# A weight stream woven through seven-product pairs: its steps placed over 28 pair steps instead of 17

## Chip, cores and metric

The kernel runs on one core of a Trainium2 chip. The metric is the device time of one execution in microseconds (us). Three runs of the kernel before gave 883.15, 884.38 and 886.47 us; the median is 884.38 us.

## What is computed

Two layers of a trunk over 256 tokens of width 2048: first a gated linear recurrence with dilated attention, then gated linear attention with a spatial gating unit, and a last norm. The change lies in the second layer. Its input projection is one product with a wide weight matrix, whose columns are then split:

```python
h = rms_norm(x, norm)
z = h @ w_in
q, k, v, a_lr, gc, u, vd, gd = jnp.split(z, split_points(ODD_SIZES), axis=-1)
...
yc = rms_norm(o, head_norm).reshape(bsz, seq, GLA_VW).astype(x.dtype) * jax.nn.silu(gc)
yd = spatial_gating(jax.nn.gelu(u), jax.nn.gelu(vd), w_s, b_s, v_norm) * jax.nn.silu(gd)
return jnp.concatenate([yc.astype(x.dtype), yd.astype(x.dtype)], axis=-1) @ w_out
```

## The kernel before

Every weight passes the same road. SP issues a load of 512 KB (128 partitions by 1024 numbers of 4 bytes) into a raw tile. ACT casts it into a high part (line 138, `whi`), DVE subtracts that from the raw tile into a low part (line 73 by way of line 139, `wlo`), and PE makes three products per operand: high by high, high by low, low by high. The rings of the high and low parts (`hip`, `lop`) have four buffers each, so ACT and DVE can be up to four pieces ahead of PE. One such piece is called a step here.

Three times (for q and k, for vd, for u) two blocks of 512 columns are made by `pair`: seven block products instead of eight, with sums of blocks as operands. A pair has 28 steps, each a cast, a subtraction and 6 matmuls of 512 columns. I number them 1 to 28:

- Steps 1 to 4 use the pieces `x0`, steps 5 to 8 the pieces `y0`, 9 to 12 `x0` again, 13 to 16 `y0`, 17 to 20 `x0`. In steps 1 to 12, as soon as a piece has been cast and subtracted, an accumulating DMA on the POOL queue (line 245) adds another block's piece to it in place; the sum is used eight steps later. So there are twelve accumulating DMAs in a pair, in three groups of four.
- Steps 21, 22, 23 and 25 use four fresh pieces `z0`, loaded into the ring called raw; steps 24, 26, 27 and 28 use `x0[0]` to `x0[3]` after DVE has added `z0[i]` to each (line 299, "the additions"). An addition is pinned by `keep_in_program_order` behind the DVE instruction that stands before it in the program: the first addition stands after step 22, then after 24, 26 and 27. Each addition ends the use of a raw buffer.
- After step 20 DVE makes four small combinations from PSUM (lines 279 to 283), and at the end a fifth (line 301). The next pair's first pieces are fetched between steps 21 and 26 (`onward`).

Beside a pair runs `Stream`: four other column blocks (the gates gc and gd) at eight steps each. A step of the stream is one piece from the raw ring, which has three buffers in all for the stream and for `z0`, and 12 matmuls of 512 columns. `weave` runs a pair and, after each of its steps, as many steps of the stream as its rule says: 10 for the first pair, 8 for the second, 10 for the third; `stream.finish` (line 982) makes the last four. When eight steps are done, ACT reads the finished block with a Silu (lines 791 and 798).

The program's order gives priorities. The framework lays out each engine's queue from them and from what it takes to be ready, except where an order is pinned. Small tasks (`spawn`, `tick`) for attention and gating are laid between the steps, by counts of products.

Of the kernel before, what the change touches and what calls it, by code (L numbers as in the profile page):

```python
# [51 lines left out]
def trunk(ctx, tc, x, xt, lead, w_in0, w_out0, w_va, w_in1, w_out1, w_gate, small, dist, cst, w_alpha, w_s,  # L52
# [164 lines left out]
    def weave(steps, stream, count):  # L217

        done = taken = 0
        while True:  # L220
            try:
                next(steps)
            except StopIteration as end:
                return end.value
            taken += 1
            while done < count and done * 17 < taken * count:
                stream.step()
                done += 1

# [573 lines left out]
    paired[0] = True  # L803
    x0 = [fetch(w_in1, 6, i, "rx") for i in range(4)]
    ps, ps_k, x0 = weave(pair(w_in1, 6, 10, act2, forms2, x0, "ry", 14), stream, 10)
    drain()
    eb, enb, ebl = decays
# [81 lines left out]
    vf = []  # L889
    mv = tiny.tile([P, 8, 2], F32, name="mv", tag="mv", bufs=1)  # L890
    *vd, x0 = weave(pair(w_in1, 14, 18, act2, forms2, x0, "rx", 30), stream, 8)
    for c, ps in enumerate(vd):
        t = big_tile([P, 2, 512], f"vf{c}")
# [53 lines left out]
    def mix(c, t):  # L947
        yield 2
        for b in range(2):
# [7 lines left out]
            yield 2  # L957

    *ud, _ = weave(pair(w_in1, 30, 34, act2, forms2, x0, "ry"), stream, 10)
    paired[0] = False  # L960
    for c, ps in enumerate(ud):
# [172 lines left out]
```

## Time and profile before

| | |
|---|---|
| median of three runs | 884.38 us |
| the profiled execution | 882.66 us |
| its span in the trace | 881.0 us |
| PE busy | 857.9 us, 97% |
| DVE busy | 610.0 us, 69% |
| ACT busy | 526.3 us, 60% |
| first pair, first matmul | 537.4 us |
| last third-pair matmuls | about 770 us |

A busy PE is not a PE at its peak, since a matmul's duration overlaps the next one's. Within the pairs it is better read by the number of matmuls in a stretch.

### The profile page before, as it was taken

To read this page: it belongs to the slowest core of one execution; us is meant where nothing else is said; L and a number is where in the kernel's file an instruction comes from. 1 tells how busy PE (TensorE), PEld (TensorE's weight loads), DVE (VectorE), ACT (ScalarE), POOL (GpSimd) and SP (SyncE) were. 2 spreads that over 40 slices of the span, in tenths; PEclk is the share of its full clock that TensorE was granted. 3 is DMA by queue.
4 is the path that set the end of the run, shared out by engine and by line. 5 is a ranking of instruction groups with operands and counts; after the bars stand their busy time and mean duration, and the time that the engine had idled before them with its cause. 6 is when DMAs were issued, how large, how long until landed. Compare 5 with 4: busy or idle time off the path is not lost.

```text
span 881.0 us, 11887 instructions
## 1 busy us (share of the span) xinstructions
PE 857.9 (97%) x4408; PEld 718.6 (82%) x4408; DVE 610.0 (69%) x867; ACT 526.3 (60%) x764; POOL 42.9 (5%) x60
## 2 busy tenths in 40 slices
PE   8999999999999999999999999998999899899996
PEld 7888888888888888888888988885768578688886
DVE  7676557677576586666555996679748976995652
ACT  7755556666766766554444776565476766654532
POOL 1100000000000000010000002201210121000000
PEclk9999999999999999999999999999999999999999
DMA  9896555555455455565544658967965899665502
GB/s 342 335 366 213 185 194 164 170 169 177 160 177 170 144 172 178 190 208 194 184 135 154 219 184 209 252 225 211 250 144 176 245 254 322 202 220 189 190 2 96
DMA packets 50266, 175.53 MB, mean 199 GB/s; under 512 B 5648, under 2 KB 6160, under 8 KB 49952
## 3 DMA queue, kind: packets, MB, share of 16 engines
q1 hardware_dynamic: 43920, 152.65, 50.8%
q0 software_dynamic: 6144, 22.06, 12.6%
q8 instruction: 34, 0.56, 0.2%
q14 instruction: 24, 0.20, 0.1%
q10 hardware_dynamic: 144, 0.07, 0.0%
HBM read 172.66 MB, written 2.10 MB: 198 GB/s over the span
## 4 chain that ended last, share of the span: by engine, by line
PE 91%; DVE 6%; ACT 1%; issue 1%; DMA 0%; ACTq 0%
PE pc L315 20%; PE ps L147 15%; PE ps L148 15%; PE ps L146 15%; PE pc L314 10%; PE ps L251 3%; PE ps L252 3%; PE ps L253 3%; DVE wlo L73 3%; ACT whi L138 1%; DVE rx L299 1%; PE pc L317 1%; PE sc L500 1%; PE gp L584 1%; PE gp L583 1%
## 5 line engine op out<-in xcount | busy, mean ns | idle before, releaser
L315 PE MATMUL pc<-act,whi 128*128 128x512 f32 x768 | 269.8, 395 | 0.0
L314 PE MATMUL pc<-act,wlo 128*128 128x256 f32 x720 | 208.5, 290 | 0.0
L73 DVE TENSOR_TENSOR wlo<-rx,whi 128x1024 fp32r<-128x1024 f32 (+2 forms) x118 | 141.4, 1199 | 74.9 <-ACT whi L138 73.3
L138 ACT CAST whi<-rx 128x1024 fp32r<-128x1024 f32 (+1 forms) x115 | 119.9, 1044 | 100.3 <-PE ps L148 59.1
L73 DVE TENSOR_TENSOR wlo<-ry,whi 128x1024 fp32r<-128x1024 f32 (+2 forms) x110 | 131.6, 1198 | 67.9 <-ACT whi L138 66.7
L315 PEld LDWEIGHTS pc<-act,whi 128*128 128x128 f32 x768 | 142.6, 188 | 29.4
L138 ACT CAST whi<-ry 128x1024 fp32r<-128x1024 f32 (+1 forms) x108 | 112.2, 1041 | 90.4 <-PE ps L148 53.2
L73 DVE TENSOR_TENSOR wlo<-raw,whi 128x1024 fp32r<-128x1024 f32 (+2 forms) x100 | 119.0, 1190 | 47.7 <-ACT whi L138 45.7
L138 ACT CAST whi<-raw 128x1024 fp32r<-128x1024 f32 (+1 forms) x97 | 100.9, 1040 | 68.0 <-PE ps L148 25.6
L314 PEld LDWEIGHTS pc<-act,wlo 128*128 128x128 f32 x720 | 135.9, 189 | 2.4 <-DVE wlo L73 0.8
L146 PE MATMUL ps<-whi,act 128*128 128x512 f32 (+2 forms) x352 | 131.8, 377 | 1.4 <-DVE la_s L473 1.1
L147 PE MATMUL ps<-wlo,act 128*128 128x512 f32 (+2 forms) x352 | 131.0, 372 | 1.3 <-DVE wlo L73 1.2
L148 PE MATMUL ps<-whi,act 128*128 128x512 f32 (+2 forms) x352 | 130.7, 371 | 0.0
L146 PE MATMUL ps<-whi,yt 128*128 128x512 f32 (+1 forms) x256 | 97.3, 380 | 0.0
L148 PE MATMUL ps<-whi,yt 128*128 128x512 f32 (+1 forms) x256 | 96.4, 376 | 0.0
L147 PE MATMUL ps<-wlo,yt 128*128 128x512 f32 (+1 forms) x256 | 96.2, 376 | 0.0
L146 PEld LDWEIGHTS ps<-whi,act 128*128 128x128 f32 x352 | 66.1, 188 | 15.0 <-issue 2.2
L147 PEld LDWEIGHTS ps<-wlo,act 128*128 128x128 f32 x352 | 66.3, 188 | 13.5 <-DVE wlo L73 2.6
L148 PEld LDWEIGHTS ps<-whi,act 128*128 128x128 f32 x352 | 66.2, 188 | 11.4
L148 PEld LDWEIGHTS ps<-whi,yt 128*128 128x128 f32 x256 | 48.2, 188 | 8.9
L147 PEld LDWEIGHTS ps<-wlo,yt 128*128 128x128 f32 x256 | 48.2, 188 | 8.5
L146 PEld LDWEIGHTS ps<-whi,yt 128*128 128x128 f32 x256 | 48.2, 188 | 8.3
(289 smaller groups left out, 1040.1 us busy)
## 6 DMA issues: line engine op xcount, KB each, us to landing
raw<-in_w_in SPq DMA_DIRECT2D x77, 512.0 KB, 5.2
ry<-in_w_in SPq DMA_DIRECT2D x64, 512.0 KB, 4.7
rx<-in_w_in SPq DMA_DIRECT2D x63, 512.0 KB, 4.6
rx<-in_w_out SPq DMA_DIRECT2D x24, 512.0 KB, 4.3
ry<-in_w_out SPq DMA_DIRECT2D x23, 512.0 KB, 4.0
rx<-in_w_in POOLq DMA_DIRECT2D x20, 512.0 KB, 9.9
raw<-in_w_out SPq DMA_DIRECT2D x17, 512.0 KB, 4.5
ry<-in_w_in POOLq DMA_DIRECT2D x16, 512.0 KB, 8.6
```

What stands on the lines that cost most here:

```text
L73: nc.vector.tensor_tensor(out=o, in0=a, in1=hi.bitcast(F32), op=ALU.subtract)
L138: nc.scalar.copy(hi, raw)
L146: nc.tensor.matmul(ps[b], xh, wh, start=first, stop=False)
L147: nc.tensor.matmul(ps[b], xh, wl, start=False, stop=False)
L148: nc.tensor.matmul(ps[b], xl, wh, start=False, stop=last)
L251: nc.tensor.matmul(ps, xh, wh, start=(first and j == 0), stop=False, skip_group_check=not first)
L252: nc.tensor.matmul(ps, xh, wl, start=False, stop=False, skip_group_check=not first)
L253: nc.tensor.matmul(ps, xl, wh, start=False, stop=(j == 7), skip_group_check=not first)
L299: tc.keep_in_program_order(nc.vector.tensor_tensor(out=x0[i - 1], in0=z0[i - 1], in1=x0[i - 1], op=ALU.add))
L314: nc.tensor.matmul(ps[c][:, 1, :], wl, act[:, k, 0:T], start=False, stop=False)
L315: nc.tensor.matmul(ps[c], wh, act[:, k, :], start=(k == 0), stop=(k == KT - 1))
L317: nc.tensor.matmul(ps[c][:, 1, :], wl, act[:, k, 0:T], start=False, stop=False)
```

## The change

Only the rule of `weave` changes:

```diff
@@ -223,7 +223,7 @@
             except StopIteration as end:
                 return end.value
             taken += 1
-            while done < count and done * 17 < taken * count:
+            while done * 28 < taken * count:
                 stream.step()
                 done += 1
```

Worked out, steps of the stream stand after these steps of a pair:

| steps of the stream | before | after the change |
|---|---|---|
| 10 (first and third pair) | 1, 2, 4, 6, 7, 9, 11, 12, 14, 16 | 1, 3, 6, 9, 12, 15, 17, 20, 23, 26 |
| 8 (second pair) | 1, 3, 5, 7, 9, 11, 13, 15 | 1, 4, 8, 11, 15, 18, 22, 25 |

The numbers of steps stay, since at step 28 the new rule has run exactly `count` of them. The pinning of the additions stands in both kernels.

## Rows read from the trace of the kernel before

**Rows 1.** The profile page: busy time by engine, granted clock, chain of work.

```profile
PE   857.9 (97%) x4408; PEld 718.6 (82%) x4408; DVE 610.0 (69%) x867; ACT 526.3 (60%) x764; POOL 42.9 (5%) x60
...
PEclk9999999999999999999999999999999999999999
...
PE 91%; DVE 6%; ACT 1%; issue 1%; DMA 0%; ACTq 0%
```

**Rows 2.** Busy time by stretch: width, each engine's busy us (instructions), clock, DMA, GB/s.

```profile
537.40:588.00 50.60, 50.60 (x225) 41.89 (x224) 32.84 (x28) 32.41 (x35) 9.42 (x11) 1.00 0.99 259
588.00:612.40 24.40, 20.27 (x80) 13.63 (x78) 23.93 (x27) 13.12 (x14) 0.85 (x1) 1.00 0.53 171
...
670.20:695.20 25.00, 20.64 (x84) 15.07 (x83) 21.92 (x24) 17.02 (x18) 0.49 (x1) 1.00 0.50 175
...
745.60:771.00 25.40, 22.41 (x91) 16.25 (x90) 23.10 (x26) 17.10 (x18) 0.00 (x0) 1.00 0.67 229
```

**Rows 3.** Timeline of PE, first pair: start, us, line; in brackets idle time and releaser.

```profile
583.66 0.39 PE L146 MATMUL ps<-whi,act 128*128 128x512 f32 x1
...
586.38 0.39 PE L251 MATMUL ps<-whi,sums 128*128 128x512 f32 x1
...
597.98 0.51 PE L251 MATMUL ps<-whi,act 128*128 128x512 f32 x1 [0.28 <-ACT whi L138]
599.75 0.50 PE L251 MATMUL ps<-whi,act 128*128 128x512 f32 x1 [1.27 <-ACT whi L138]
...
605.12 0.50 PE L252 MATMUL ps<-wlo,act 128*128 128x512 f32 x1 [0.69 <-DVE wlo L73]
```

**Rows 4.** Groups of DVE instructions, 588.9 to 612.9 us: count, busy, mean ns, idle.

```profile
L73 DVE TENSOR_TENSOR wlo<-raw,whi 128x1024 fp32r<-128x1024 f32 x5 | 6.1, 1219 | 0.3
L299 DVE TENSOR_TENSOR rx<-raw,rx 128x1024 f32<-128x1024 f32 x4 | 4.9, 1216 | 0.0
...
L813 DVE SCALAR_TENSOR_TENSOR enb<-t,rs,enb 128x512 f32<-128x512 f32 x1 | 0.7, 742 | 0.0
...
L279 DVE TENSOR_TENSOR t<-ps,s 128x512 f32<-128x512 f32 x1 | 0.7, 683 | 0.0
```

**Rows 5.** Timeline of ACT, end of the first pair.

```profile
581.13 1.05 ACT L138 CAST whi<-rx 128x1024 fp32r<-128x1024 f32 x1 [1.21 <-PE ps L148]
...
586.58 1.05 ACT L138 CAST whi<-rx 128x1024 fp32r<-128x1024 f32 x1 [1.66 <-PE ps L148]
...
592.85 1.05 ACT L138 CAST whi<-rx 128x1024 fp32r<-128x1024 f32 x1 [1.14 <-DVE rx L299]
596.87 1.05 ACT L138 CAST whi<-raw 128x1024 fp32r<-128x1024 f32 x1 [2.97 <-DMA raw<-in_w_in]
```

**Rows 6.** Loads into the raw ring, three short stretches: issue start, then time to landing.

```profile
L214 SPq DMA_DIRECT2D raw<-in_w_in x1: 328/328/328, 569.9 to 569.9; - x1
...
DMA to landing us min/median/max: 7.9/7.9/7.9
...
L214 SPq DMA_DIRECT2D raw<-in_w_in x1: 328/328/328, 592.8 to 592.8; - x1
...
DMA to landing us min/median/max: 4.0/4.0/4.0
...
L214 SPq DMA_DIRECT2D raw<-in_w_in x1: 327/327/327, 735.0 to 735.0; - x1
...
DMA to landing us min/median/max: 11.7/11.7/11.7
```

**Rows 7.** Busy time by stretch, for the DMA share (last but one column).

```profile
545.00:585.00 40.00, 40.00 (x178) 33.12 (x177) 25.97 (x23) 26.39 (x27) 7.14 (x9) 1.00 1.04 271
585.00:590.00 5.00, 5.00 (x23) 4.13 (x22) 3.37 (x3) 2.81 (x3) 0.00 (x0) 1.00 0.31 125
...
745.00:751.00 6.00, 6.00 (x28) 4.97 (x27) 4.24 (x5) 3.17 (x3) 0.00 (x0) 1.00 0.78 311
751.00:755.00 4.00, 4.00 (x19) 3.27 (x18) 4.00 (x5) 2.01 (x2) 0.00 (x0) 1.00 0.38 129
```

**Rows 8.** Third group of accumulating DMAs (line 245), first and third pair: issue, landing.

```profile
L245 POOL DMA_DIRECT2D rx<-in_w_in x4: 847/856/881, 560.5 to 570.9; - x4
...
DMA to landing us min/median/max: 10.0/10.1/11.0
...
L245 POOL DMA_DIRECT2D rx<-in_w_in x4: 847/861/866, 719.9 to 731.9; - x4
...
DMA to landing us min/median/max: 10.3/10.5/11.7
```

**Rows 9.** Timeline of ACT, third pair: the casts that use that third group.

```profile
740.34 1.05 ACT L138 CAST whi<-rx 128x1024 fp32r<-128x1024 f32 x1 [1.66 <-PE ps L148]
...
745.78 1.05 ACT L138 CAST whi<-rx 128x1024 fp32r<-128x1024 f32 x1 [1.66 <-PE ps L148]
```

**Rows 10.** Line 791, all its instructions: ns min/median/max, first and last start.

```profile
L791 ACT ACTIVATE sgc<-ps,rs x4: 682/684/689, 575.3 to 660.4; 128x512 f32<-128x512 f32 x4
L791 ACT ACT_TABLE_LOAD x2: 1283/1283/1283, 574.0 to 658.5; - x2
```

**Rows 11.** Timeline of DVE, start of the third pair: a run of small operations.

```profile
707.49 0.20 DVE L331 RECIPROCAL rv<-rv 128x8 f32<-128x8 f32 x1 [1.08 <-ACT rv L330]
...
711.88 0.40 DVE L936 TENSOR_SCALAR vf<-vf,mv,rv 128x256 f32<-128x256 f32 x1
...
713.34 0.68 DVE L938 TENSOR_TENSOR vf<-vf,vn 128x512 f32<-128x512 f32 x1
```

## The prediction

> **What bounds the kernel now.** I read the page first: PE is busy 97% of the span at the full granted clock (2.4 GHz), and 91% of the chain of work that ended last is PE [rows 1]. A kernel whose chain is PE gains only where PE stands still, so the next view is busy time by stretch. From the first pair's first matmul at 537.4 us to 588 us PE ran 225 matmuls in 50.6 us, without a gap, while DVE was busy 32.8 us, 65% [rows 2]. Then come 24.4 us in which PE ran 80, with DVE busy 23.9 us, 98% [rows 2]. The bound changes inside a pair: PE first, DVE in the last eight steps, called the tail here. The other pairs have the same tail: 84 matmuls in 25.0 us, 91 in 25.4 us [rows 2].
>
> How much PE loses there follows from its pace. The stream's step that began at 583.66 and the pair's step 17 at 586.38 are 12 matmuls apart: 2.72 us, so 0.227 us each, 1.36 us for a pair's step [rows 3]. The three tails at that pace would take 80 x 0.227 = 18.1, 19.1 and 20.6 us; what is left is 6.3, 5.9 and 4.8 us of standing still, 17.0 us in all. This is the most the change can give back. The gaps name who ends them: ACT's cast and DVE's subtraction, in turn [rows 3].
>
> Why DVE is late in the tail: each of steps 21 to 28 costs it a subtraction (1.22 us), four steps also an addition (1.22), and five combinations (0.68) and, in the first pair, six scalings (0.74) come on top [rows 4]. That is 8 x 1.22 + 4 x 1.22 + 5 x 0.68 + 6 x 0.74 = 22.5 us against 8 x 1.36 = 10.9 us of PE. All the stream's steps, each 2.72 us of PE for one subtraction, lie before step 17, where DVE had room.
>
> **The change, part by part.** No instruction is added or removed; steps of the stream move. In pairs one and three four of ten now follow step 17 or later (after 17, 20, 23, 26), in pair two three of eight (after 18, 22, 25).
>
> *Throughput.* The tail from step 17 gains 4 x 2.72 = 10.9 us of PE work (8.2 in pair two) and 4 x 1.22 = 4.9 us of DVE work. DVE's 22.5 + 4 x 1.22 (steps 17 to 20) + 4.9 = 32.3 us then stands against PE's 12 x 1.36 + 10.9 = 27.2 us, less a start of four pieces: the cast of step 17 began at 581.13, 5.2 us ahead of PE [rows 3, 5]. By throughput alone the 17.0 us come back nearly whole.
>
> *The raw ring.* It does not stop there, because the stream and z0 share three raw buffers, and each z0 piece holds its buffer until its addition. In the kernel before, the last stream piece was loaded long before z0[3] needed a buffer, and yet that load waited for the first addition: issued at 592.8, landing 4.0 us later, and ACT stood 3.0 us for it [rows 5, 6]. Now two stream pieces ask too. I lay out the first tail by hand, with step 17 on PE at 0, a load 4.0 [rows 6], a cast 1.05 [rows 5], a subtraction or an addition 1.2 at most [rows 4], and step 24 taken ahead where it is ready first. Step 22's subtraction ends at 9.3 (four pieces behind PE's release), the first combination at 9.9, the first addition at 11.0. The stream's piece after step 23 loads into the buffer freed there: landed 15.1, cast 16.2, low part 17.4; PE could begin it at 16.3 and needs the low part one matmul later, so it waits 0.85. The second addition ends at 15.6; z0[3] lands at 19.7, low part 22.0, PE there at 21.3: 0.5. The stream's piece after step 26 takes the buffer freed at 17.4, lands at 22, low part 24.2, PE there at 23.2: 0.8. The third addition is pinned behind that subtraction, so cast and subtraction of step 27 end at 27.7, PE there at 26.7: 0.8. Then the fourth addition, cast, subtraction: 31.2, PE there at 29.4 with the next pair's first step laid before it: 1.4. Together 4.3 us. Behind the waiting cast on ACT, and behind the pinned addition on DVE, stand the next casts and subtractions; PE is who waits. The ends: 3.5 if the next pair's pieces fill more of it, 6.5 if the queues keep the program's order (step 24 behind the stream's piece, which delays the second addition and all after it).
>
> So tail one goes from 6.3 to 4.3: 2.0 gained. In pair two the stream's piece after step 22 finds a buffer freed by the piece after 18, and only one piece (after 25) depends on an addition: I take 2.5 (1.5 to 4.5) for 5.9, 3.5 gained. Tail three is tail one with loads that land later (735.0: 11.7 us [rows 6]) and the unit's activations beside it: I take 4.8 for 4.8, nothing.
>
> *The Silu.* The first block is complete after step 20 instead of 12, so a table load and two activations (1.28 + 2 x 0.68 us [rows 10]) move into the tail on ACT. ACT is busy only 13.1 of 24.4 us there [rows 2] and would wait for the load in any case: nothing, or 1 us if it delays a cast that is due; inside the range.
>
> *The accumulating DMAs.* With fewer stream steps between steps 1 and 16, sums are due sooner. Nothing on POOL's queue changes its order, and SP's fetches of the stream only move back. The third group was issued from 560.5 to 570.9 and landed 10.0 to 11.0 us later; the casts that read it began from 581.13 to 586.58: spare 10.6 us for the first, 4.6 for the last [rows 5, 8]. In the third pair: 8.7 and, at the median landing, 3.4 [rows 8, 9]. The way from step 9 to 17 loses two stream steps (5.4 us), that from 12 to 20 none. The queue grows: by step 12 the issues come three stream steps, 8.2 us, closer, while three loads fewer are moved, each 0.524 MB / 271 GB/s = 1.9 us at the saturated rate [rows 7]; that is 2.4 us for the last, 1.6 for the first. Spare is then 3.6 and 2.2 us, in pair three 1.7 and 1.0. Thin, but no wait: nothing, to 2 us less of the start that ACT and DVE have.
>
> *The start of the next pair.* At the third pair's start DVE spends 707.5 to 714.0 us on small operations [rows 11]. Of four pieces ahead of PE two were the stream's, 8.2 us of cover; now 1.4 on average, 7.3 us. I take 1.0 us lost (0 to 1.6); the tasks laid by `tick` move a little with the products and cost nothing more.
>
> Sum: -2.0 - 3.5 + 0 + 1.0 = -4.5 us. The profiled execution took 882.7 us, 1.7 of it outside the span; it would take 878.2. The median stands 1.7 above it, so 879.9 us.
>
> **The rivals.**
>
> *Whole refund.* The queues are laid out so that other pieces fill every gap, and only the 1.0 us at the start of pair three is lost: 884.4 - 17.0 + 1.0 = 868.4; down from the forecast it covers 866 to 876. For it: DVE has the room, 17.8 us idle before 588 [rows 2]. Against: the chain through the raw ring, which a wait of 3.0 us shows already [rows 5]. The Trainium skill (Perfetto Trace Analysis, Optimization Strategy) says that where the most-contended engine changes over time, interleaving the regimes may improve performance; by that rule alone the time would be this rival's.
>
> *The wait changes its name.* Program order is kept, tails one and three stand 6.5 us and tail two 4.5: +0.2, +1.7, -1.4, and 1.0 at the start: 884.4 + 1.5 = 885.9. That the new rule does nothing, since the layout restores the old interleaving, would give 884.4 and is counted here.
>
> *Slower: the raw loads land late.* One mechanism: the loads of the tail, now chained behind additions, meet DMA engines that still drain the accumulating DMAs and the prefetches. Their landing takes 7.9 to 11.7 us then instead of 4.0 [rows 6], and two stand in series, so a tail grows by 8 us or more. It decides where the engines are not drained by step 22. In pair one they were drained at 585 (share 1.04, then 0.31 [rows 7]) and step 22 would be at 587.7; in pair three they were at 0.78 until 751 [rows 7], where step 22 would come at about 747. So tail three is the place: -2.0 - 3.5 + 8 + 1.0 = +3.5, 888; with tail one as well 898. The Trainium skill (DMA: Bandwidth & Descriptors, Issuing engines are not separate DMA queues) says that transfers of all issuing engines run on the same 16 engines and interleave, which speaks for this; the trace's 4.0 against 11.7 us agrees.
>
> **How the numbers follow.** The forecast (877 to 882) has 0.42, the whole refund 0.22, the changed wait 0.20, the late loads 0.16. The range goes from 868 to 890: it holds the refund down to its worked-out time and the late loads in one tail, and leaves out some 0.1 above and 0.05 below. A measurement of this kernel can tell about 0.5% from no change, 4.4 us: faster means under 880.0. The refund and somewhat over half of the forecast lie there: 0.46; the rest of the forecast and most of the changed wait are within: 0.36; the late loads and a bad end of the changed wait: 0.18.
>
> **What would show it.** In the profile after: stretches before step 17 still without a gap on PE, with DVE's share up a little; matmuls of the stream (lines 146 to 148) between those of lines 251 to 253 in the tails; PE standing 4.3, 2.5 and 4.8 us in the tails, ended by ACT's cast; ACT waiting several times for DMA of raw, where it waited once. Waits of ACT for rx or ry by DMA would mean the sums came late. The prediction is wrong if the tails stand under 1 us each (the ring did not bind), or if tail three stands over 10 us.

## The result and the profile after

The changed kernel takes 899.33 us (median; 897.95 to 900.66), the kernel before 884.6 us in the runs beside it: a ratio of 1.0173 [1.0156, 1.0191]. It is slower by 15 us where I had forecast 4.5 us less. The profiled execution has a span of 896.5 us against 881.0.

The page of the kernel after, four of its rows (busy time by engine, granted clock in 40 slices, chain of work by engine and by line):

```profile
PE   867.7 (97%) x4408; PEld 724.3 (81%) x4408; DVE 610.3 (68%) x867; ACT 525.9 (59%) x764; POOL 42.4 (5%) x60
...
PEclk9999999999999999999999999999998999899998
...
PE 82%; DMA 8%; DVE 4%; issue 2%; ACT 2%; POOL 0%; ACTq 0%; POOLq 0%; DVEq 0%; SPq 0%
PE pc L315 20%; PE ps L146 13%; PE ps L148 13%; PE ps L147 13%; PE pc L314 10%; DMA raw<-in_w_in 6%; DVE wlo L73 2%; PE ps L251 2%; PE ps L252 2%; PE ps L253 2%; ACT whi L138 2%; DMA rx<-in_w_in 1%; DVE rx L299 1%; PE pc L317 1%; PE sc L500 1%
```

PE is still 97% busy with the same 4408 matmuls, so that row says nothing. The chain does: DMA had 0% of it [rows 1] and has 8% now, 6% of it the loads into the raw ring. And PE's clock, without a dip on the page before [rows 1], shows dips.

Where the time went is read at one mark per pair, the fifth combination (line 301) at its end. DVE's timeline, that line, kernel before:

```profile
610.48 0.68 DVE L301 TENSOR_TENSOR s<-ps,s 128x512 f32<-128x512 f32 x1
695.36 0.68 DVE L301 TENSOR_TENSOR s<-ps,s 128x512 f32<-128x512 f32 x1
768.98 0.69 DVE L301 TENSOR_TENSOR s<-ps,s 128x512 f32<-128x512 f32 x1
```

and kernel after:

```profile
612.52 0.68 DVE L301 TENSOR_TENSOR s<-ps,s 128x512 f32<-128x512 f32 x1
703.02 0.68 DVE L301 TENSOR_TENSOR s<-ps,s 128x512 f32<-128x512 f32 x1
784.85 0.69 DVE L301 TENSOR_TENSOR s<-ps,s 128x512 f32<-128x512 f32 x1
```

Pair one ends 2.0 us later; from its end to that of pair two it is 90.5 us instead of 84.9, +5.6; pair three takes 81.8 instead of 73.6, +8.2. What follows the last mark is 0.4 us shorter. All of the loss lies in the pairs.

Busy time by stretch, kernel after (width, then PE, PEld, DVE, ACT and POOL busy with instructions, clock, DMA share, GB/s). The first rows answer to [rows 2]; the last four are the stretches within the pairs in which the granted clock was at its lower level (it was there in the last 6 us of the span too, and in the last 3 before):

```profile
537.40:588.00 50.60, 50.60 (x225) 41.90 (x224) 35.33 (x30) 31.90 (x33) 9.42 (x11) 1.00 0.93 239
588.00:614.00 26.00, 21.67 (x81) 15.21 (x80) 22.26 (x25) 13.78 (x16) 0.86 (x1) 0.93 0.62 201
672.00:705.00 33.00, 26.05 (x93) 18.85 (x92) 23.59 (x29) 17.06 (x19) 0.85 (x1) 0.90 0.50 161
745.00:787.00 42.00, 35.26 (x132) 25.41 (x131) 28.27 (x32) 20.95 (x22) 0.00 (x0) 0.92 0.64 221
...
593.63:597.04 3.41, 3.41 (x9) 2.64 (x9) 3.41 (x5) 0.00 (x0) 0.00 (x0) 0.50 0.65 192
682.38:685.79 3.41, 3.11 (x7) 2.23 (x7) 3.41 (x4) 2.43 (x3) 0.00 (x0) 0.50 0.11 40
692.62:696.03 3.41, 3.41 (x9) 2.66 (x9) 2.29 (x3) 1.98 (x3) 0.00 (x0) 0.50 0.58 178
764.30:771.10 6.80, 6.03 (x14) 4.60 (x15) 3.50 (x3) 2.17 (x3) 0.00 (x0) 0.50 0.46 144
```

Before 588 us nothing is lost: 225 matmuls as before, with DVE 2.5 us busier. In the tails DVE, 98% busy before [rows 2], is now at 22.3 of 26.0 us, 23.6 of 33.0 and 28.3 of 42.0. It was relieved, and yet PE stands longer. At 0.227 us for a matmul PE loses 26.0 - 81 x 0.227 = 7.6 us, 33.0 - 93 x 0.227 = 11.9 and 42.0 - 132 x 0.227 = 12.0, 31.5 in all against 17.0 before. That is 14.5 of the 15.5 us.

What the first tail waits for stands in four timelines of the kernel after. SP's queue, then DVE, ACT and PE (start, us, engine and line; in brackets idle time and its releaser):

```profile
587.34 0.33 SPq L132 DMA_DIRECT2D raw<-in_w_in  x1
593.40 0.33 SPq L214 DMA_DIRECT2D raw<-in_w_in  x1
...
595.68 0.33 SPq L132 DMA_DIRECT2D raw<-in_w_in  x1
```

```profile
586.06 1.22 DVE L299 TENSOR_TENSOR rx<-raw,rx 128x1024 f32<-128x1024 f32 x1
...
592.15 1.22 DVE L73 TENSOR_TENSOR wlo<-raw,whi 128x1024 fp32r<-128x1024 f32 x1 [1.09 <-ACT whi L138]
593.30 1.22 DVE L73 TENSOR_TENSOR wlo<-rx,whi 128x1024 fp32r<-128x1024 f32 x1
594.43 1.22 DVE L299 TENSOR_TENSOR rx<-raw,rx 128x1024 f32<-128x1024 f32 x1
```

```profile
591.08 1.04 ACT L138 CAST whi<-raw 128x1024 fp32r<-128x1024 f32 x1 [1.61 <-DVE s L283]
592.03 1.04 ACT L138 CAST whi<-rx 128x1024 fp32r<-128x1024 f32 x1
597.59 1.05 ACT L138 CAST whi<-raw 128x1024 fp32r<-128x1024 f32 x1 [4.52 <-PE ps L148]
...
600.94 1.05 ACT L138 CAST whi<-raw 128x1024 fp32r<-128x1024 f32 x1 [1.35 <-DMA raw<-in_w_in]
604.49 1.05 ACT L138 CAST whi<-rx 128x1024 fp32r<-128x1024 f32 x1 [2.50 <-DVE rx L299]
```

```profile
592.17 0.73 PE L146 MATMUL ps<-whi,act 128*128 128x512 f32 x2 [1.73 <-ACT whi L138]
```

Read it as one chain. The first addition (586.06 to about 587.3) frees a raw buffer, and at 587.34 SP issues the stream's load (line 132) into it. It takes 3.7 us. ACT casts that piece at 591.08, and PE, which had stood 1.73 us, goes on at 592.17. The cast of step 24 (`rx`, made ready by the first addition at 587.3) stands behind it in ACT's queue and runs at 592.03. DVE subtracts the stream's piece at 592.15 to 593.4, which frees its buffer: z0[3] is issued at 593.40 and takes 4.1 us. The second addition is pinned behind step 24's subtraction, and so behind the stream's: it runs at 594.43, though the z0 piece that it reads had been cast and subtracted before the first addition began. The buffer that it frees carries the next stream load at 595.68, which takes 5.2 us. So the first load, of 3.7 us, holds up the other two, of 4.1 and 5.2 us: both are released by DVE work that stands behind its piece, and the last lands 13.6 us after the first addition's end. (Two waits carry other names. The 1.61 us ahead of 591.08 are put down to a combination of DVE that ended with the landing, the 4.52 us ahead of 597.59 to a matmul of PE that ended about 0.1 us after the landing at 597.49. In the run heat28 below the same two casts wait for the loads by name, 1.20 and 4.06 us.)

ACT's waits for loads, by stretch (engine and line, releaser: us in total, times, longest), kernel after, from 530 to 620, 620 to 710 and 710 to 810 us:

```profile
ACT whi L138 <- DMA raw<-in_w_in: 4.4, 4, 1.4
...
ACT whi L138 <- DMA rx<-in_w_in: 2.1, 1, 2.1
...
ACT whi L138 <- DMA raw<-in_w_in: 9.5, 3, 7.5
...
ACT whi L138 <- DMA raw<-in_w_in: 15.2, 5, 5.8
ACT whi L138 <- DMA rx<-in_w_in: 5.6, 3, 2.8
```

Before, the waits for raw loads were one of 3.0 us in the first pair [rows 5], one of 2.8 in the second and two of 4.2 together in the third: 10.0 us against 29.1. The sums (`rx`) are late too: once in pair one, 2.1 us for step 20, where PE did not stand, and three times in pair three.

### The profile page after: what moved, and what is told of

It reads as the page before. It is cut to its first block, busy times and chain, and to the rows that moved or that the text cites. A ratio compares the mean times of both kernels' runs of the same rounds, so it can differ in the third digit from the quotient of the medians.

```text
span 896.5 us, 11877 instructions
## 1 busy us (share of the span) xinstructions
PE 867.7 (97%) x4408; PEld 724.3 (81%) x4408; DVE 610.3 (68%) x867; ACT 525.9 (59%) x764; POOL 42.4 (5%) x60
## 4 chain that ended last, share of the span: by engine, by line
PE 82%; DMA 8%; DVE 4%; issue 2%; ACT 2%; POOL 0%; ACTq 0%; POOLq 0%; DVEq 0%; SPq 0%
PE pc L315 20%; PE ps L146 13%; PE ps L148 13%; PE ps L147 13%; PE pc L314 10%; DMA raw<-in_w_in 6%; DVE wlo L73 2%; PE ps L251 2%; PE ps L252 2%; PE ps L253 2%; ACT whi L138 2%; DMA rx<-in_w_in 1%; DVE rx L299 1%; PE pc L317 1%; PE sc L500 1%
## 5 line engine op out<-in xcount | busy, mean ns | idle before, releaser
L146 PE MATMUL ps<-whi,act 128*128 128x512 f32 (+2 forms) x352 | 133.5, 384 | 7.3 <-ACT whi L138 6.9
L147 PE MATMUL ps<-wlo,act 128*128 128x512 f32 (+2 forms) x352 | 133.7, 380 | 0.8 <-DVE wlo L73 0.8
L148 PE MATMUL ps<-whi,act 128*128 128x512 f32 (+2 forms) x352 | 133.3, 379 | 0.0
L146 PEld LDWEIGHTS ps<-whi,act 128*128 128x128 f32 x352 | 67.1, 192 | 22.2 <-ACT whi L138 8.8
L148 PEld LDWEIGHTS ps<-whi,act 128*128 128x128 f32 x352 | 67.7, 192 | 11.9 <-issue 0.3
```

The costliest lines, as they stand in the source:

```text
L146: nc.tensor.matmul(ps[b], xh, wh, start=first, stop=False)
L147: nc.tensor.matmul(ps[b], xh, wl, start=False, stop=False)
L148: nc.tensor.matmul(ps[b], xl, wh, start=False, stop=last)
```

## The experiments

**The ring.** If the shared ring makes the chain, z0 in another ring must set the spreading free. The four z0 pieces are loaded ahead of step 21 into the ring of `y0`, and the next pair's first pieces are fetched after the additions:

```diff
-        z0 = []
+        z0 = [fetch(w, ua + 2, i, tag) for i in range(4)]
         for i in range(6):
             if i < 4:
-                z0.append(fetch(w, ua + 2, i, "raw"))
                 step(m12, (act, 8, 0), i, z0[i], False)
                 yield
-                if after is not None:
-                    onward.append(fetch(w, after, i, tag))
...
                 tc.keep_in_program_order(...)   # the addition
+                if after is not None:
+                    onward.append(fetch(w, after, i - 1, tag))
```

With the rule at 28:

> The changed kernel (28 steps), with the four z0 pieces loaded into the ring of y0, whose buffers are free after step 16, all four at once ahead of step 21; the next pair's first pieces are fetched into that ring as each addition frees a buffer. The stream then has the raw ring's three buffers to itself. Theory A (the tail's loads are chained behind additions because stream and z0 share three raw buffers; the standing PE then also falls to the lower clock level): ACT no longer waits for raw in the tails, PE stands under 3 us in each, granted clock 1.0 through the pairs, time 868 to 882 us. Rival B (the accumulating DMAs come closer together, and sums and loads land late because the DMA engines are full): the same bytes move at the same places, so 894 to 900 us. Rival C (the queues keep the program's order, and the pinned additions with their casts are the chain, whatever the ring): 888 to 898 us.

Measured: 875.29 us, ratio 0.9906 [0.9889, 0.9923], 24.0 us under the kernel after. (The kernel before, run beside each group of experiments, had medians from 883.65 to 884.7 us; a difference between groups is uncertain by as much.) And the control, the same edit with the rule at 17:

> The kernel before (17 steps) with the same edit: z0 in the ring of y0. Theory A: there the ring cost only the 3.0 us that ACT waited for z0[3] in a tail already bound by DVE, so 880 to 885 us, and clearly slower than the same edit at 28 steps. Rival B and C: 883 to 886 us, and faster than the same edit at 28 steps.

Measured: 883.26 us, 0.9997 [0.9988, 1.0006]. The edit alone brings nothing; with it, spreading the stream gains 8.0 us. The three tails of z28, busy time by stretch:

```profile
588.00:608.00 20.00, 18.65 (x81) 14.27 (x80) 19.74 (x23) 12.01 (x14) 0.00 (x0) 1.00 0.71 245
665.00:692.00 27.00, 24.18 (x99) 17.87 (x98) 23.90 (x30) 18.67 (x21) 0.80 (x1) 1.00 0.53 186
740.00:762.00 22.00, 21.61 (x95) 17.20 (x94) 21.15 (x24) 14.57 (x16) 0.00 (x0) 1.00 0.76 265
```

PE loses 20.0 - 81 x 0.227 = 1.6, 4.5 and 0.4 us there, 6.5 instead of 31.5; DVE is at 99%, 89% and 96% again, and the clock at 1.00. ACT does not wait for a raw load once in these pairs; for sums it still waits twice, 4.0 us. With z0 out of the ring no raw load waits for an addition, and the chain is gone. The edit does three things at once: z0 leaves the ring, its loads are issued earlier, and the next pair's first pieces later. They weren't tried one by one.

**The clock.** The lower level might have been a cause of its own. Three matmuls that nobody reads are pinned on PE after each of steps 22 to 27, to fill the gaps:

```diff
+        warmer = bank()
+
+        def keep_warm():
+            for _ in range(3):
+                tc.keep_in_program_order(nc.tensor.matmul(warmer, act[:, 1, 0:P], act[:, 0, :], start=True, stop=True))
```

> The changed kernel with three idle matmuls (128x512, into a spare PSUM bank that nobody reads) pinned on PE behind each of steps 22 to 27: 18 per pair, 4.1 us of PE work each pair, which fits into waits where PE stands. If the fall of the granted clock to 0.5 behind the long waits is a cause of its own: granted clock 1.0 in the tails and 889 to 896 us. If the clock is no cause: 899 to 905 us.

Measured: 899.22 us, 1.018 [1.016, 1.0201], the same as the kernel after. The first tail of heat28, busy time by stretch, and then two casts of ACT's timeline:

```profile
588.00:614.00 26.00, 23.36 (x94) 16.59 (x93) 21.02 (x24) 12.64 (x15) 0.82 (x1) 1.00 0.55 190
```

```profile
591.08 1.05 ACT L138 CAST whi<-raw 128x1024 fp32r<-128x1024 f32 x1 [1.20 <-DMA raw<-in_w_in]
...
597.14 1.05 ACT L138 CAST whi<-raw 128x1024 fp32r<-128x1024 f32 x1 [4.06 <-DMA raw<-in_w_in]
```

The clock is back at 1.00 here and in pair three (0.995 over the whole span, against 0.987 after); in pair two it still fell once, for 3.41 us. z0[3] is cast at 597.14 where it was 597.59: the loads set the pace at either clock. The idle matmuls are 54 x 0.227 = 12.3 us of PE work that had to fit into the waits, so a gain of the clock of a few us could be hidden under what of them did not fit. That the clock cost nothing is not shown. But of the 17.0 us at half the clock in the pairs of the kernel after at most half, 8.5 us, can be lost to it, and with most of them gone the time is the same.

**The accumulating DMAs.** Left out here are the twelve additions of other blocks per pair that DMA makes in place (line 245):

```diff
-            if u is not None:
+            if False:
                 nc.gpsimd.dma_start(out=raw, in_=piece_of(w, u, i), accum_op=ALU.add)
```

From the kernel after:

> The changed kernel without the twelve accumulating DMAs of each pair (line 245), so that steps 9 to 20 use pieces that lack the added block. Theory A: the waits for raw in the tails of pairs one and two stay (their loads landed in 3.6 to 5 us anyway), only pair three's early loads land sooner: 892 to 899 us. Rival B: the cause is gone, 870 to 885 us.

Measured: 889.85 us, 1.0068 [1.0044, 1.0091], between the two ranges, so neither account alone: 9.5 us less, of which 6.8 in pair three (75.0 us from mark to mark instead of 81.8). From the kernel before, as control:

> The kernel before without the twelve accumulating DMAs of each pair (steps 9 to 20 use pieces that lack the added block): the control for noacc28 (889.9 us). If sums and loads were never late at 17 steps: 882 to 885 us. If the accumulating DMAs cost time there too: 876 to 880 us, and the gain of noacc28 is then not the change's.

Measured: 883.56 us, 0.9996 [0.9983, 1.0009], nothing. So what these DMAs cost at 28 is no cost that they always have. DMA issues where z0 of pair three is loaded (KB each, median us from issue to landing), kernel after from 736 to 742 us:

```profile
q0 software_dynamic: 220, 0.83, 69.3%
...
raw<-in_w_in SPq DMA_DIRECT2D x2, 512.0 KB, 15.0
fn<-in_r_fnorm POOLq DMA_DIRECT2D x2, 512.0 KB, 12.8
```

noacc28, from 729 to 742 us:

```profile
raw<-in_w_in SPq DMA_DIRECT2D x3, 512.0 KB, 4.7
```

A raw load took 15.0 us while POOL's queue (q0, with the accumulating DMAs and the two prefetches `fn` of the last norm) held 69% of the engines, and 4.7 without them. The edit also let the two `fn` loads be issued at 652 us, far ahead of this place, so what of the 6.8 us is theirs and what the sums' isn't shown. Some 6 us over the kernel before remain without these DMAs, most of them in pair two (90.2 us from mark to mark instead of 84.9): I read them as the chain.

**The place of the stream's steps.** With 22 in the rule of before, no step of the stream falls between the z0 pieces: the last stand after step 20.

```diff
-            while done < count and done * 17 < taken * count:
+            while done < count and done * 22 < taken * count:
```

> The kernel before with 22 in the rule instead of 17 (ten steps of the stream after steps 1, 3, 5, 7, 9, 12, 14, 16, 18, 20; eight after 1, 3, 6, 9, 12, 14, 17, 20): spread further than before, but none of them between the z0 pieces. Raw ring of three, shared, as in both kernels. Theory A (loads of the stream and of z0 chained behind additions in the shared ring): no chain forms, so no long wait for raw in tails one and two, 876 to 884 us. If spreading itself were the harm (sums due sooner, B): between the two kernels, 888 to 895 us.

Measured: 881.03 us, 0.9958 [0.9943, 0.9972]. A spreading that stays clear of z0 gains 3.7 us, although ACT still waits nine times for raw loads, 16.7 us in all. I put the loss of the change down to the two steps of the stream per pair that stand among the z0 pieces (after 23 and 26, after 22 and 25). This run alone doesn't show it, since the other steps moved too; z28 has all steps of the change at their places, and no loss.

**The pin.** The other link of the chain is DVE's order. First without it:

```diff
-                tc.keep_in_program_order(nc.vector.tensor_tensor(out=x0[i - 1], in0=z0[i - 1], in1=x0[i - 1],
-                                                                 op=ALU.add))
+                nc.vector.tensor_tensor(out=x0[i - 1], in0=z0[i - 1], in1=x0[i - 1], op=ALU.add)
```

> The changed kernel with the four additions not pinned in DVE's order. Rival C (the pinning holds the additions, and with them the raw buffers, behind the stream's late pieces): 884 to 892 us. Theory A without C: an addition needs its own z0 piece cast and subtracted and its x0 piece read, which is what it waits for already, so 896 to 902 us.

Measured: 886.59 us, 1.0024 [1.0014, 1.0033]. It is 12.7 us better than the kernel after and no better than before: additions are then laid too early. DVE's timeline of nopin28:

```profile
581.19 1.23 DVE L299 TENSOR_TENSOR rx<-raw,rx 128x1024 f32<-128x1024 f32 x1 [7.36 <-DMA raw<-in_w_in]
```

DVE stood 7.36 us for a load that the addition reads, with subtractions queued behind it. Then pinned still, but ahead of the stream's piece: the block of the addition moves up, between the step of `m12` and its `yield`:

```diff
                 step(m12, (act, 8, 0), i, z0[i], False)
+            if 0 < i < 5:
+                tc.keep_in_program_order(...)   # the addition
+            if i < 4:
                 yield
...
-            if 0 < i < 5:
-                tc.keep_in_program_order(...)   # the addition
```

> The changed kernel with each addition one or two steps sooner in the program: behind the subtraction of the next z0 piece and ahead of the stream's piece (after steps 22, 23, 25 and 26, before the stream's turn), still pinned. Theory A: buffers come free sooner by one subtraction and, for the second to fourth, by one or two pieces, so the chain of loads shortens by 2 to 4 us per tail: 888 to 894 us. If the loads are not what sets the tail: 897 to 901 us.

Measured: 887.51 us, 1.0034 [1.0021, 1.0046], just under the expected range and 11.8 us better than after. Pair one ends at 606.0 us, 4.5 earlier than before; pairs two and three are 3.5 and 3.6 us longer than before. In pair one additions that stand a step or two sooner are nearly enough; in the others the shared ring still costs, as the next run shows.

**Both.** z0 in the ring of `y0` and the additions sooner, at 28:

> z0 in the ring of y0 (as in z28, 875.3 us) and the additions sooner (as in early28), at 28 steps. With no shared ring, what is left of the tails' standing is the chain addition, cast, subtraction on the pieces x0 (about 2 us a tail in z28); sooner additions shorten it: 870 to 874 us. If that chain is hidden anyway: 874 to 877 us.

Measured: 873.62 us, 0.9873 [0.9852, 0.9894], the best of all, 11.1 us under the kernel before. Against early28 z0 out of the ring takes 2.1 us off pair one, 5.0 off pair two and 7.4 off pair three. Its tails, busy time by stretch:

```profile
584.00:604.00 20.00, 20.00 (x89) 16.28 (x88) 19.96 (x22) 14.03 (x15) 0.00 (x0) 1.00 0.70 242
665.00:688.00 23.00, 21.10 (x91) 16.40 (x90) 21.56 (x28) 16.45 (x19) 0.47 (x1) 1.00 0.53 179
735.00:757.00 22.00, 20.85 (x92) 16.76 (x91) 21.86 (x23) 15.62 (x18) 0.00 (x0) 1.00 0.74 264
```

PE loses 0, 2.3 and 1.1 us: of the 17.0 us of before 13.6 came back in the tails, 10.8 in the span. Two more runs place it. The same edits at 17:

> z0 in the ring of y0 and the additions sooner, at 17 steps: the control for zearly28 (873.6 us). If spreading the stream is what gains once the loads are free: 880 to 883 us here. If ring and additions alone gain: 873 to 876 us.

Measured: 880.28 us, 0.9963 [0.9948, 0.9977]; and at 24:

> As zearly28 with 24 in the rule: the stream's last steps at step 22 instead of 26. If the best place is even spreading: 874 to 877 us; if the tail has room to spare at 28 and the sums are due too soon there: 871 to 873 us.

Measured: 877.12 us, 0.9926 [0.9904, 0.9948]. So with the loads free the spreading itself is worth 6.7 us from 17 to 28 (7.5 if each is set against the kernel before beside it), and less than half of that (3.2) is there at 24; the even spacing is the best of the three.

The gains over the kernel after (24.0 by the ring, 18.3 by the place, 12.7 and 11.8 by the pin, 9.5 by the sums) add up to far more than the loss, so they are not separate costs: the first four, as I read them, break the same chain at different links. A larger ring for the stream and z0 together wasn't tried.

## Why the prediction was wrong

**What held.** The stretch before 588 us lost nothing. The tails were DVE's before, and the moved steps did relieve it. The raw ring was named as what stands between the change and the refund, and its waits of ACT came, where I looked for them. The refund existed: z28 and zearly28 fall into the range of the first rival, 866 to 876. The Trainium skill (Perfetto Trace Analysis, Optimization Strategy) says that interleaving regimes may help; zearly17 against zearly28, 880.3 to 873.6 us, agrees, and the change as made, 884.6 to 899.3, shows that it need not. The same section of the Trainium skill says that bubbles which repeat can mean too few buffers for the next tile; here z28 agrees, which lends the z0 pieces four buffers of another ring, by 24.0 us; early28 gets 11.8 from the same buffers, freed sooner.

**The step that failed first: "step 24 taken ahead where it is ready first".** The layout of tail one rested on that. The queues kept the program's order: step 24's cast, ready at 587.3, ran at 592.03, behind the stream's. I had it as an upper end (6.5 us of standing). The tail stood 7.6 us, of which at most 1.7 can be the clock's (3.41 us of the tail ran at its lower level, half the pace). So the end that I gave a lesser weight was about right, and the middle, 4.3, wrong. By the same step I had z0[3] in the buffer of the second addition; it took that of the stream's piece, and the second addition came after it. From the end of the first addition the load of z0[3] landed after 10.2 us instead of my 8.7, the next stream's after 13.6 instead of 11.0. Over the three tails I was out by 3.3, 9.4 and 7.2 us; these 19.9 us are the whole miss, from 4.5 us faster to 15 slower.

**The term that was most mis-sized: tail two**, 2.5 us of standing (1.5 to 4.5), and it stood 11.9 (2.47 and 2.90 us in the two gaps below, at most 3.4 by the clock, the rest in smaller gaps). I had one dependent load there, the stream's. The timelines of ACT, PE, SP and DVE, kernel after:

```profile
669.16 1.28 ACT L791 ACT_TABLE_LOAD   x1
...
671.61 1.99 ACT L138 CAST whi<-raw 128x1024 fp32r<-128x1024 f32 x2
681.09 1.04 ACT L138 CAST whi<-raw 128x1024 fp32r<-128x1024 f32 x1 [7.49 <-DMA raw<-in_w_in]
...
690.34 1.04 ACT L138 CAST whi<-raw 128x1024 fp32r<-128x1024 f32 x1 [1.07 <-DMA raw<-in_w_in]
```

```profile
682.19 0.65 PE L251 MATMUL ps<-whi,act 128*128 128x512 f32 x1 [2.47 <-ACT whi L138]
...
691.43 0.74 PE L146 MATMUL ps<-whi,act 128*128 128x512 f32 x2 [2.90 <-ACT whi L138]
```

```profile
677.11 2.66 SPq L214 DMA_DIRECT2D raw<-in_w_in  x2
```

```profile
673.52 0.69 DVE L279 TENSOR_TENSOR t<-ps,s 128x512 f32<-128x512 f32 x1 [0.68 <-PE ps L253]
...
675.87 1.22 DVE L73 TENSOR_TENSOR wlo<-raw,whi 128x1024 fp32r<-128x1024 f32 x1
...
678.20 1.22 DVE L299 TENSOR_TENSOR ry<-raw,ry 128x1024 f32<-128x1024 f32 x1
```

Not only the stream's pieces stand behind z0; z0 stands behind the stream's piece as well. The piece after step 22 did find its buffer, as I had it, but it then held the one that z0[2] needed. z0[2] was issued at 677.11, when the subtraction of that piece (675.87) freed its buffer, and landed 3.9 us later; ACT had stood 7.49. The first addition, pinned behind the same subtraction, ran only at 678.20. The second gap is the one that I counted. The Silu with its table load, in the prediction "nothing, or 1 us", was laid at 669.16, directly ahead of two casts; that it cost anything isn't shown. Both casts were over at 673.6, and DVE's queue had the two subtractions that need them (674.13 and 675.87) behind a combination that waited for PE until 673.52. No run took the Silu away.

**Tail three, "4.8 for 4.8, nothing"**, stood 12.0 us, and the step **"thin, but no wait"** on the accumulating DMAs fell here: the spare of 1.0 to 1.7 us was less than nothing, ACT waited 5.6 us for sums, and the raw loads issued at 736.95 and 741.27 landed 15.4 and 14.5 us later, beyond the 11.7 of [rows 6]. This is the slower rival, at the place that it named, and noacc28, which moves the `fn` loads as well, puts 6.8 us on it (my price was 8). The chain was in this tail too: ACT's two longest waits, 5.78 us ahead of 763.98 and 4.63 ahead of 770.60, were for loads issued late, at 760.02 behind the first addition and at 766.30 behind the stream's subtraction, that landed in 3.9 and 4.2 us. The Trainium skill (DMA: Bandwidth & Descriptors, Issuing engines are not separate DMA queues), that transfers of all issuers run on the same engines and interleave, agrees with 15.0 against 4.7 us.

**Where that rival was wrong** is its point of decision, undrained DMA engines. Pairs one and two lost 7.6 us together although the tails' loads named above landed in 3.7 to 5.2 us: a chain of loads costs time even when each is prompt. I held rival two (order kept) and rival four (late loads) for alternatives; they came together. By the sum: tails 1.3 + 6.0 + 7.2 where I had -2.0 - 3.5 + 0; elsewhere in the pairs 1.3 us (I had 1.0); after them -0.4: 15.4 of the 15.5 us. Rival four "with tail one as well" gave 898 us, nearly the time, but for half the wrong reason, so that was luck, and the range ended at 890 because I counted the mechanisms one at a time.

## What to carry to other kernels

Before a second consumer is woven between steps that share a small ring of buffers, write down for every load which instruction frees its buffer and what that instruction is queued or pinned behind; if that is again the subtraction of a loaded piece, loads run in series, and each costs its whole time to landing, as the 3.7 us here did with the DMA engines at a share of 0.29. Assume that in-order queues keep the program's order when a layout is worked out by hand, and add mechanisms that hit different stages instead of choosing among them. Moving work away from a bound engine paid here in full only once its loads had buffers of their own (z28), and in part where it stayed clear of the other loads (rule22).

## What the hardware showed unexpectedly

TensorE's granted clock fell from 2.4 to 1.2 GHz (1.00 to 0.50) for 3.41 to 6.8 us shortly after PE had stood for 1.7 to 2.9 us (ahead of 592.17, 682.19 and 691.43), and in the fourth place during the second of two stands of 1.8 and 1.9 us (761.74 and 765.07). The row from 593.63 to 597.04 counts nine matmuls in 3.41 us, where the pace of 0.227 us gives fifteen. In the kernel before, with gaps up to 1.6 us in the tails (ahead of 759.04), it did not fall within the pairs. In nopin28 it fell for 10.2 us in one place, in which PE ran 13 matmuls. And the same 512 KB load took 3.7 us with the DMA engines at a share of 0.29 (from 585 to 590 us) and 15.4 us among accumulating DMAs and prefetches, in one and the same execution.
